# Layer norms of a transformer layer: VectorE reads the spread rows of 1/std and mean from PSUM

## The chip, the cores and the metric

The kernel runs on one core of one Trainium2 chip. The time is the device time of one execution in microseconds; less is better. The profile is one profiled execution on that core.

## The reference

One layer of a diffusion backbone on 1024 tokens of width 1024, all in fp32: modulation, two attention mixers (windowed and global) merged by gates, and a ConvFFN. Each of the two sublayers ends in a residual sum and a layer norm, which is the part that the change touches:

```
def _layer_norm(x, g, b):
    mu = mean(x, axis=-1)
    var = mean(square(x - mu), axis=-1)
    return (x - mu) * rsqrt(var + LN_EPS) * g + b

x = _layer_norm(DEEPNORM_ALPHA * x + gate1 * y, ln1_g, ln1_b)     # y: attention mixers
h = x * (1 + scale2) + shift2
u = conv1d(h @ w_up) + conv_b                                     # width 3, per channel
y = (silu(u_gate) * u_val) @ w_down
x = _layer_norm(DEEPNORM_ALPHA * x + gate2 * y, ln2_g, ln2_b)
```

## The kernel before

Activations lie transposed: features on the 128 partitions (8 tiles f = 0..7), tokens along the free dimension. A matrix product in fp32 is three matmuls on a high and a low fp32r part (`mm3`, L88 to L90); `split` makes the parts, the high one by a cast (L80) and the low one by a subtraction (L85).

A layer norm has to reduce over partitions. For a slice s of tokens, `ln_steps` (L1013) returns a list of steps. `stats`: matmuls of the running sums zs and zq against a column of ones give token sums (tile st), from which VectorE, with one power on GpSimd, makes rs = 1/std and mr = mean x rs per token. `diags`: VectorE multiplies the identity by rs and by mr (tiles dgr, dgm). `cast`: a matmul of ones against these spreads each row over all 128 partitions in PSUM (tiles bcr and bcm, or both halves of one tile bc where the slice has 256 tokens), and ScalarE copies each into SBUF (rb and mb, L1045). `apply(f)`, eight times: VectorE multiplies the tile z (zz in the second norm) by rb (L1050), VectorE or GpSimd subtracts mb (L1052), and `emit` does the rest. The argument pm says who subtracts: GpSimd where (f + 1) is a multiple of pm.

The first norm has three slices, LN1_S: tokens 0 to 511, 512 to 767, 768 to 1023, with pm = 2 throughout and the order f = 0, 4, 1, 5, 2, 6, 3, 7. It runs beside the matmuls of the attention's output projection (y_pair, tile y; its eviction is L1060) and of the first up-projection tiles (tile u). `emit1` stores a residual zo to the DRAM tensor zd (by ScalarE, or by GpSimd at L1094 for odd f), writes the high part B (L1068), and the low part by a subtraction on VectorE or GpSimd (L1074). Then `build` makes sums of tiles (t, T13, T24), on the same engines, for the following fast products.

The second norm has the slices LN2_S, of the same sizes. The first two use `ln_steps`, with pm from LN2_P; the third goes another way (token-major, tiles zt and stl) and is not touched. The first half, "b0", runs beside product 5 of the down-projection (tile p). `emit2` scales and shifts on ScalarE (tile of, L1407) and stores to the output (L1408). Then follow the products yl of the last quarter of the down-projection, one slice of 256 tokens after the other, each four feature tiles over 11 pairs of weights. Seven pairs are loaded early; the other four are cast by ScalarE (L80) and VectorE (L85) in a ring of four pairs of buffers that product 5 also uses. `accum` (L1414) evicts p and yl into zz on VectorE, and `sums` (L993, L994) updates zs and zq.

What sets the order: TensorE's instructions go in the order of the program (a manual schedule); the steps of a norm are put between matmuls by a clock of due times (`pend`, `tick`, LN1_F, LN1_D, LN2_D, LN2_E). On the other engines a planner orders the instructions by its own costs. Each engine then works its queue in order. [...]

Of the kernel before, what the change touches and what calls it, by code (L numbers as in the profile page):

```python
# [7 lines left out]
F32 = mybir.dt.float32  # L8
R32 = mybir.dt.float32r
AF = mybir.ActivationFunctionType  # L10
ALU = mybir.AluOpType
AX = mybir.AxisListType

P = 128
# [13 lines left out]
HALF = 512  # L28
# [26 lines left out]
PSU = 6, 7, 2, 3, 4, 5, 0, 1  # L55
PSO = 4, 5, 0, 1, 7, 6, 2, 3
UE = "vector", "vector", "vector", "vector", "vector", "gpsimd", "gpsimd"
LN2_P = 1, 2, 2
GAP = 1
LN1_S = slice(0, 512), slice(512, 768), slice(768, 1024)  # L60
VOFF = 0.0
# [6 lines left out]
def layer_kernel(  # L68
# [6 lines left out]
    nc = tc.nc  # L75
# [55 lines left out]
    def ht(name, shape=(P, T), dt=F32):  # L131
        hslot[name] = pool, tag = hfree.pop(0)
        return pool.tile(list(shape), dt, tag=tag, name=name, bufs=1)
# [71 lines left out]
    def modulate(k):  # L205
        wm, x, wr = st1.pop(k)
        w = wsplit(wr, f"qb{k}")
        for j in (0, 1):
            col = j * 8 + k
            mod(wm[j], sc, bmc[:, col:col + 1], modc[:, col:col + 1])  # L210
        hh = hTp.tile([P, T], R32, tag="hT", name=f"hh{k}", bufs=16)
        hl = hTp.tile([P, T], R32, tag="hT", name=f"hl{k}", bufs=16)
        a, b = modc[:, k:k + 1], modc[:, 8 + k:9 + k]
        for s in [slice(0, HALF), slice(HALF, T)] if k == 0 else [slice(0, T)]:
            nc.scalar.activation(hh[:, s], x[:, s], AF.Identity, bias=a, scale=b)
            nc.scalar.activation(x[:, s], x[:, s], AF.Identity, bias=a, scale=b)
            nc.vector.tensor_tensor(out=hl[:, s], in0=x[:, s], in1=hh[:, s].bitcast(F32), op=ALU.subtract)
        hT.append((hh, hl))
        return w
# [7 lines left out]
    w = modulate(0)  # L227
    for k in range(KT):
# [8 lines left out]
        w = wn  # L237
# [461 lines left out]
    for n, (gi, k) in enumerate(order):  # L699
# [9 lines left out]
        nm, src, tiles = groups[gi]  # L709
# [3 lines left out]
        w, c = ready.pop((gi, k))  # L713
        for t in tiles:
            if t < NT:
                s = slice(t * P, (t + 1) * P)
                a = hT[k][0][:, s], hT[k][1][:, s]
            else:
                s = slice((t - NT) * P, (t - NT + 1) * P)
                a = c[0][:, s], c[1][:, s]  # L720
# [161 lines left out]
    def big(name):  # L882
        return ps3.tile([P, T], F32, tag="big", name=name, bufs=3)

    def sml(name, w=512):
        return ps3.tile([P, w], F32, tag="sml", name=name, bufs=2)
# [28 lines left out]
    def zv(f, s):  # L915
        hf = s.start // HALF
        return zt_[f % 4, hf][:, f // 4, s.start - hf * HALF:s.stop - hf * HALF]
# [24 lines left out]
    for f in range(2, KT):  # L942
        bT[1, f] = ht(f"bT1_{f}")
        nc.sync.dma_start(bT[1, f], sgd[KT + f])
        w = wb[f // 2]
        ps = big(f"b1_{f}")
        for j in range(4):
            k = (f % 2) * 4 + j
            for hf in (0, 1):
                a = O[1, hf, 0, j // 2][:, j % 2], O[1, hf, 1, j // 2][:, j % 2]  # L950
# [9 lines left out]
    post = tc.alloc_tile_pool(name="post", bufs=1, side="left", reuse_waits="tile")  # L960
# [8 lines left out]
    def tiny(name):  # L969
        return post.tile([P, 8], F32, tag="tiny", name=name, bufs=6)  # L970

    def diag(cols, n, nm):
        dg = tm(f"dg{nm}", w=HALF).rearrange("p (a b) -> p a b", b=P)
        nc.vector.tensor_tensor(out=dg[:, 0:n], in0=ident.unsqueeze(1).to_broadcast([P, n, P]),
                                in1=cols.unsqueeze(2).to_broadcast([P, n, P]), op=ALU.mult)
        return dg[:, 0:n].rearrange("p a b -> p (a b)")
# [3 lines left out]
    def ln_flush():  # L980
        while sqs:
            sqs.pop(0)()
# [30 lines left out]
    def ln_steps(zs, zq, s, nm, emit, first, gap, gap1, gap2, each, pm=2, order=range(KT)):  # L1013
        w = s.stop - s.start
        n = w // P
        bcs = []
        sv = []

        def stats():
            ln_flush()  # L1020
            sv.extend(tiny(f"{a}{nm}") for a in ("mv", "m2", "rs", "mr"))
            mv, m2, rs, mr = sv
            st = sml(f"st{nm}")
            for t in range(n):
                ts = slice(s.start + t * P, s.start + (t + 1) * P)
                nc.tensor.matmul(st[:, t:t + 1], zs[:, ts], onec, start=True, stop=True)
                nc.tensor.matmul(st[:, n + t:n + t + 1], zq[:, ts], onec, start=True, stop=True)
            nc.vector.tensor_scalar(out=mv[:, 0:2 * n], in0=st[:, 0:2 * n], scalar1=1.0 / D, scalar2=None,
                                    op0=ALU.mult)
            nc.vector.tensor_tensor(out=m2[:, 0:n], in0=mv[:, 0:n], in1=mv[:, 0:n], op=ALU.mult)  # L1030
            nc.vector.scalar_tensor_tensor(out=rs[:, 0:n], in0=mv[:, n:2 * n], scalar=LN_EPS, in1=m2[:, 0:n],
                                           op0=ALU.add, op1=ALU.subtract)
            nc.gpsimd.tensor_tensor(out=rs[:, 0:n], in0=rs[:, 0:n], in1=mhalf[:, 0:n], op=ALU.pow)
            nc.vector.tensor_tensor(out=mr[:, 0:n], in0=mv[:, 0:n], in1=rs[:, 0:n], op=ALU.mult)

        def diags():
            bcs.extend(diag(c[:, 0:n], n, f"{a}{nm}") for a, c in zip("rm", sv[2:]))

        def cast():
            both = sml(f"bc{nm}") if 2 * w <= HALF else None  # L1040
            for i, a in enumerate("rm"):
                ps = sml(f"bc{a}{nm}")[:, 0:w] if both is None else both[:, i * w:(i + 1) * w]
                nc.tensor.matmul(ps, onesf, bcs[i], start=True, stop=True)
                o = post.tile([P, HALF], F32, tag="mrs", name=f"{a}b{nm}", bufs=2)[:, 0:w]
                nc.scalar.copy(o, ps)  # L1045
                bcs[i] = o

        def apply(f):
            zf = zv(f, s)
            nc.vector.tensor_tensor(out=zf, in0=zf, in1=bcs[0], op=ALU.mult)  # L1050
            e = nc.vector if (f + 1) % pm else nc.gpsimd
            e.tensor_tensor(out=zf, in0=zf, in1=bcs[1], op=ALU.subtract)  # L1052
            emit(f, s)

        return [(first, stats), (gap, diags), (gap1, cast)] + [(gap2 if n == 0 else each, lambda f=f: apply(f))
                                                for n, f in enumerate(order)]

# [421 lines left out]
    for p in (1, 6, 2, 7, 4, 5):  # L1479
# [35 lines left out]
        if p == 4:  # L1515
            after.append(lambda: pend.extend(ln_steps(zs2, zq2, h0, "b0", emit2, *LN2_D, LN2_P[0])))
    yb, ab = sides[nside[0] % 2], sides[nside[0] % 2 ^ 1]
# [10 lines left out]
    w = s.stop - s.start  # L1528
    nt = w // P

    def pst(n, name):
        return ps4.tile([P, HALF], F32, tag=f"r{n}", name=name)
# [50 lines left out]
    zt[0] = [pst(n, f"zt0_{n}") for n in yb[0:2]]  # L1583
    pend += ln_steps(zs2, zq2, r, "b1", emit2, *LN2_E, LN2_P[1])
    r = LN2_S[2]
    for f, done_ in enumerate(((4, 5), (6, 7, 0), (1,), (2, 3))):
        o = pst(yb[2 + f % 2], f"yl{f}_{r.start}")[:, 0:w]
# [15 lines left out]
    for t, a in OTO:  # L1603
        o = ot[t, a] = ht(f"ot{t}_{a}", (P, HALF))
        nc.vector.scalar_tensor_tensor(out=o, in0=lnr[0][:, a], scalar=mv[:, t:t + 1], in1=zt[a][t], op0=ALU.mult,
                                       op1=ALU.add)
    for t, a in OTO:
        o = ot[t, a]
# [125 lines left out]
```

## Time and profile before

| | |
|---|---|
| median of 3 runs | 1618.45 us (1617.10 to 1619.27) |
| profiled execution, first to last instruction | 1618.4 us; no other time of it is recorded, and this stands level with the median |
| TensorE busy | 1545.6 us, 95% |
| VectorE busy | 1199.0 us, 74% |
| ScalarE busy | 816.8 us, 50% |
| GpSimd busy | 746.4 us, 46% |
| granted TensorE clock, mean | 0.987 |

In the profile PE is TensorE (PEld its weight loads), DVE is VectorE, ACT is ScalarE, POOL is GpSimd and SP is SyncE, which issues most DMAs. "out<-in" are the program's names without numbers, and L1050 is line 1050 of the kernel. A row of a timeline has the start in us, the duration, engine, line, operation, operands and, in brackets, the idle time before it and what ended it. A row of a group has busy us and mean ns of one, then the idle time before. Matmuls are pipelined: a matmul's duration is longer than the distance to the next one's start.

### The profile page before, as it was taken

The page shows a single profiled execution, that of the slowest core. Times are in us where ns is not written, and L with a number is a line of the kernel's source. Part 1 is how long each engine was busy: PE and PEld are TensorE (multiplying, and loading weights), DVE is VectorE, ACT ScalarE, POOL GpSimd, SP SyncE. Part 2 cuts the span into 40 slices and gives each one's busy share as a digit, 9 for nine tenths or more (in the row PEclk, how much of TensorE's full clock was granted, in tenths as well). Part 3 has the DMA queues.
Part 4 walks back from the last instruction along what each step waited for, and adds up shares of the span by engine and source line. Part 5 has one row for each costly group of instructions (what it writes and reads, how often), then busy time and mean ns, then how long its engine had stood idle before and what let it go on. Part 6 is the DMA issues. An engine that isn't in the chain of part 4 may idle for free.

```text
span 1618.4 us, 22204 instructions
## 1 busy us (share of the span) xinstructions
PE 1545.6 (95%) x7748; PEld 1283.5 (79%) x7748; DVE 1199.0 (74%) x1764; ACT 816.8 (50%) x1455; POOL 746.4 (46%) x731
## 2 busy tenths in 40 slices
PE   6999999999999999999999988999999999999987
PEld 5878788888877887777788876888888888888877
DVE  7797646538887777888765786588888788658883
ACT  5422122458887667788332563444444444436542
POOL 0583302526666556555333444566667764111131
PEclk9999999999999999999999999999999999999997
DMA  9695662322246655520540313123334447996711
GB/s 377 218 322 179 212 203 85 124 72 60 63 132 146 148 126 129 119 63 19 196 169 18 109 46 116 66 105 104 117 105 118 115 119 202 342 268 228 230 64 53
DMA packets 112369, 230.00 MB, mean 142 GB/s; under 512 B 12961, under 2 KB 27809, under 8 KB 112161
## 3 DMA queue, kind: packets, MB, share of 16 engines
q1 hardware_dynamic: 96816, 198.93, 36.6%
q0 software_dynamic: 10400, 20.19, 8.1%
q10 hardware_dynamic: 5040, 9.46, 1.6%
q8 instruction: 61, 1.00, 0.2%
q14 instruction: 52, 0.42, 0.1%
HBM read 177.35 MB, written 65.86 MB: 150 GB/s over the span
## 4 chain that ended last, share of the span: by engine, by line
PE 78%; DVE 9%; ACT 4%; issue 4%; POOL 3%; DMA 2%; SPq 0%; DVEq 0%; ACTq 0%; POOLq 0%
PE ptr L529 5%; PE p L88 4%; PE p L89 4%; PE p L90 3%; PE g L88 3%; PE g L89 3%; PE g L90 3%; PE b L90 3%; PE b L89 3%; PE b L88 3%; PE c L88 2%; PE c L89 2%; PE c L90 2%; PE d L89 2%; PE d L90 2%
## 5 line engine op out<-in xcount | busy, mean ns | idle before, releaser
L539 DVE TENSOR_TENSOR ptl<-ptr,pth 128x512 fp32r<-128x512 f32 x188 | 124.8, 685 | 27.9 <-ACT pth L538 25.2
L529 PE MATMUL ptr<-ident,p 128*128 128x128 f32 x816 | 126.5, 278 | 10.1 <-DVE ptl L539 7.7
L538 ACT CAST pth<-ptr 128x512 fp32r<-128x512 f32 x188 | 106.5, 588 | 56.4 <-PE ptr L529 32.6
L85 DVE TENSOR_TENSOR ld<-rd,hd 128x1024 fp32r<-128x1024 f32 x77 | 94.2, 1241 | 51.1 <-ACT hd L80 49.0
L424 ACT ACTIVATE p<-p,nm 128x1024 f32<-128x1024 f32 (+2 forms) x128 | 125.4, 982 | 10.9 <-DVE p L457 10.1
L529 PEld LDWEIGHTS ptr<-ident,p 128*128 128x128 f32 x816 | 93.7, 140 | 40.1 <-DVE ptl L539 13.4
L80 ACT CAST hd<-rd 128x1024 fp32r<-128x1024 f32 x77 | 79.3, 1051 | 81.7 <-PE p L90 51.1
L550 PE MATMUL av<-pth,VT 128*128 128x512 f32 x236 | 104.6, 443 | 1.0 <-ACT avs L556 0.5
L88 PE MATMUL p<-hd 128*128 128x512 f32 x264 | 103.2, 391 | 0.0
L90 PE MATMUL p<-hd,ld 128*128 128x512 f32 x264 | 102.7, 389 | 0.0
L89 PE MATMUL p<-ld,hd 128*128 128x512 f32 x264 | 102.7, 389 | 0.0
L88 PE MATMUL g<-hh,whg 128*128 128x512 f32 x256 | 99.9, 390 | 0.0
L90 PE MATMUL g<-hh,wlg 128*128 128x512 f32 x256 | 99.8, 390 | 0.0
L551 PE MATMUL av<-ptl,VT 128*128 128x512 f32 x236 | 97.7, 414 | 2.0 <-POOL ptl L85 1.9
L89 PE MATMUL g<-hl,whg 128*128 128x512 f32 x256 | 99.6, 389 | 0.0
L85 POOL TENSOR_TENSOR wlg<-wg,whg 128x512 fp32r<-128x512 f32 x32 | 45.1, 1415 | 109.9 <-ACT whg L80 109.9
L457 DVE TENSOR_SCALAR_CACHE_REDUCE p<-s,cvt,nmc 128x1024 f32<-128x1024 f32 x64 | 84.4, 1339 | 12.4 <-PE s L413 12.0
L412 PE MATMUL s<-KL,q 128*128 128x512 f32 (+2 forms) x192 | 76.1, 396 | 2.9 <-ACT p_x L424 2.0
L186 DVE CUSTOM_DVE_ANT_0 wml<-wml,sc,bmc 128x1024 f32<-128x1024 f32 x32 | 45.0, 1418 | 39.7 <-DMA wml<-in_wmodT_dram 38.2
L82 POOL TENSOR_SCALAR pth<-prw 128x512 fp32r<-128x512 f32 x48 | 31.1, 647 | 88.3 <-ACT prw L535 62.7
L413 PE MATMUL s<-KL,q 128*128 128x512 f32 (+2 forms) x192 | 71.7, 373 | 0.0
L80 ACT CAST wA<-ru 128x512 fp32r<-128x512 f32 x57 | 35.5, 623 | 71.5 <-PE d L90 34.1
(420 smaller groups left out, 5022.9 us busy)
## 6 DMA issues: line engine op xcount, KB each, us to landing
wml<-in_wmodT_dram SPq DMA_DIRECT2D x48, 512.0 KB
ru<-in_w_up_dram SPq DMA_DIRECT2D x38, 512.0 KB
rd<-td SPq DMA_DIRECT2D x55, 256.0 KB
rd<-sd SPq DMA_DIRECT2D x44, 256.0 KB
rd<-in_w_dn_dram SPq DMA_DIRECT2D x33, 256.0 KB
wm<-in_wmodT_dram SPq DMA_DIRECT2D x16, 512.0 KB
wg<-in_w_g_dram SPq DMA_DIRECT2D x32, 256.0 KB
sgd<-sg ACTq DMA_DIRECT2D x32, 256.0 KB
```

The costliest lines, as they stand in the source:

```text
L80: nc.scalar.copy(hi, src)
L85: lo_eng.tensor_tensor(out=lo, in0=src, in1=hi.bitcast(F32), op=ALU.subtract)
L88: nc.tensor.matmul(ps, a[0], b[0], start=start, stop=False, skip_group_check=resumed)
L89: nc.tensor.matmul(ps, a[0], b[1], start=False, stop=False, skip_group_check=resumed)
L90: nc.tensor.matmul(ps, a[1], b[0], start=False, stop=stop, skip_group_check=resumed)
L424: nc.scalar.activation(p, s, AF.Exp, bias=nm[:, h:h + 1], scale=scale, accum_out=sm[:, h:h + 1])
L457: nc.vector.tensor_scalar(out=p, in0=o, scalar1=self.qscale(nqs)[:, hs] if self.br else -1.0, scalar2=self.other[:, hs], op0=ALU.mult, op1 ...
L529: nc.tensor.transpose(tr[:, h * P:(h + 1) * P], self.pslice(h, n), ident)
L538: nc.scalar.copy(hi, tr)
L539: nc.vector.tensor_tensor(out=lo, in0=tr, in1=hi.bitcast(F32), op=ALU.subtract)
L550: nc.tensor.matmul(self.av, v, hi, start=first, stop=False)
L551: nc.tensor.matmul(self.av, v, lo, start=False, stop=self.left == 0)
```

## The change

ScalarE no longer copies the spread row of 1/std: VectorE multiplies by it straight from PSUM. The spread mean row is still copied to SBUF, after both matmuls, since GpSimd subtracts from there; VectorE's own subtractions read it from PSUM. In the second norm's first half pm goes from 1 to 2: the four even tiles are subtracted on VectorE and the four odd ones on GpSimd, where all eight were on GpSimd. The tag "mrs" in SBUF, with two buffers, now takes one tile per norm slice instead of two.

```
-LN2_P = 1, 2, 2
+LN2_P = 2, 2, 2
...
             for i, a in enumerate("rm"):
                 ps = sml(f"bc{a}{nm}")[:, 0:w] if both is None else both[:, i * w:(i + 1) * w]
                 nc.tensor.matmul(ps, onesf, bcs[i], start=True, stop=True)
-                o = post.tile([P, HALF], F32, tag="mrs", name=f"{a}b{nm}", bufs=2)[:, 0:w]
-                nc.scalar.copy(o, ps)
-                bcs[i] = o
+                bcs[i] = ps
+            mean = post.tile([P, HALF], F32, tag="mrs", name=f"mb{nm}", bufs=2)[:, 0:w]
+            nc.scalar.copy(mean, bcs[1])
+            bcs.append(mean)

         def apply(f):
             zf = zv(f, s)
             nc.vector.tensor_tensor(out=zf, in0=zf, in1=bcs[0], op=ALU.mult)
-            e = nc.vector if (f + 1) % pm else nc.gpsimd
-            e.tensor_tensor(out=zf, in0=zf, in1=bcs[1], op=ALU.subtract)
+            if (f + 1) % pm:
+                nc.vector.tensor_tensor(out=zf, in0=zf, in1=bcs[1], op=ALU.subtract)
+            else:
+                nc.gpsimd.tensor_tensor(out=zf, in0=zf, in1=bcs[2], op=ALU.subtract)
             emit(f, s)
```

## The prediction

> **What bounds the kernel now.** I read the chain that ended last first, then the list of who waited for whom on TensorE, then the timelines around the two layer norms.
>
> ```profile
> span 1618.4 us, 22204 instructions
> ...
> PE 78%; DVE 9%; ACT 4%; issue 4%; POOL 3%; DMA 2%; SPq 0%; DVEq 0%; ACTq 0%; POOLq 0%
> ```
>
> TensorE carries 78% of the chain, so outside TensorE's idle gaps a faster VectorE or GpSimd is worth nothing. The gaps that touch the norms are these, in the columns total us, times, longest:
>
> ```profile
> PE yl L88 <- DVE zz L1414: 4.5, 1, 4.5
> PE u L88 <- DVE c L1233: 3.0, 1, 3.0
> PE sta L1026 <- DVE zs L993: 2.8, 1, 2.8
> PE u L89 <- DVE B L1074: 1.4, 1, 1.4
> PE u L89 <- POOL B L1074: 1.3, 1, 1.3
> PE bca L1043 <- ACT rba L1045: 1.3, 2, 0.8
> PE bcb L1043 <- ACT rbb L1045: 0.5, 1, 0.5
> ```
>
> The sum is 14.8 us, 0.9% of the span: this is nearly all the change can win directly. The largest lies behind the second norm's first half. Its timeline (start, duration, engine; "x8" is eight in a row):
>
> ```profile
> 1545.29 11.50 DVE L1050 TENSOR_TENSOR zz<-zz,rbb 128x512 f32<-128x512 f32 x8 [0.53 <-ACT rbb L1045]
> 1546.19 13.00 POOL L1052 TENSOR_TENSOR zz<-zz,mbb 128x512 f32<-128x512 f32 x8 [7.69 <-ACT mbb L1045]
> 1545.53 0.59 ACT L1045 COPY mbb<-bcmb 128x512 f32<-128x512 f32 x1 [0.27 <-PE bcmb L1043]
> 1559.23 0.82 ACT L1407 ACTIVATE of<-zz,ln2c 128x512 f32<-128x512 f32 x1 [0.44 <-POOL zz L1052]
> 1559.95 3.88 ACT L80 CAST hd<-rd 128x1024 fp32r<-128x1024 f32 x4
> 1561.01 4.63 DVE L85 TENSOR_TENSOR ld<-rd,hd 128x1024 fp32r<-128x1024 f32 x4 [2.32 <-ACT hd L80]
> 1574.91 0.48 DVE L1414 SCALAR_TENSOR_TENSOR zz<-yl,nmod,zz 128x256 f32<-128x256 f32 x1
> 1554.90 0.28 PE L88 MATMUL yl<-hd 128*128 128x256 f32 x1
> 1570.61 0.28 PE L90 MATMUL yl<-hd,ld 128*128 128x256 f32 x1
> 1575.44 0.58 PE L88 MATMUL yl<-hd 128*128 128x256 f32 x1 [4.55 <-DVE zz L1414]
> 1580.72 0.35 PE L88 MATMUL yl<-hd 128*128 128x256 f32 x1
> ```
>
> All eight subtractions run on GpSimd, back to back, 13.00/8 = 1.63 us each. ScalarE writes each feature tile out behind its subtraction, so the eighth output leaves at 1559.23, and only then do the four casts of the last weights start, in order behind it. VectorE, idle for 2.32 us, gets its first low part at 1561.01 and works off its backlog until it evicts the third accumulator at 1574.91. TensorE needs that bank and stands still from 1570.9 to 1575.44. GpSimd's subtractions thus set a gap 12 us later.
>
> The gap has a tail, seen in the granted clock (after the busy times: PEclk, DMA share, GB/s):
>
> ```profile
> 1574.00:1581.00 7.00, 5.56 (x26) 5.56 (x27) 3.36 (x9) 1.25 (x3) 0.00 (x0) 0.51 0.00 0
> 1585.00:1591.00 6.00, 6.00 (x30) 6.00 (x30) 0.06 (x1) 0.00 (x0) 0.00 (x0) 0.50 0.01 3
> ```
>
> After the gap TensorE gets half its clock: 25 matmuls take 1580.72 - 1575.44 = 5.28 us, where the same shape starts every 0.12 us before the gap (1554.90 to 1570.61 in 131 steps). That is 5.28 - 25 x 0.12 = 2.3 us more. The second slow stretch stands behind small statistics matmuls, not behind this gap, and I leave it as it is.
>
> **Why the operations are slow.** A multiply of the second norm takes 11.50/8 = 1.44 us. The nearest row of a VectorE subtraction that reads one input from PSUM, with GpSimd busy beside it, is the softmax stage's (min/median/max ns, then three in a row, then GpSimd's neighbour with its mean):
>
> ```profile
> L539 DVE TENSOR_TENSOR ptl<-ptr,pth x188: 652/686/695, 353.1 to 773.0; 128x512 fp32r<-128x512 f32 x188
> 400.08 1.88 DVE L539 TENSOR_TENSOR ptl<-ptr,pth 128x512 fp32r<-128x512 f32 x3
> L85 POOL TENSOR_TENSOR ptl<-prw,pth 128x512 fp32r<-128x512 f32 x48 | 63.4, 1320 | 2.6
> L1052 DVE TENSOR_TENSOR z<-z,mba 128x512 f32<-128x512 f32 x4 | 2.6, 683 | 0.0
> ```
>
> Not one of 188 is stretched (maximum 695 ns) and three take 1.88 us, so 0.60 us each in a row. The norm's multiply and GpSimd's subtraction both read two SBUF tensors, and both are stretched (1.44 against 0.69, 1.63 against 1.32): they hold each other up. With the row in PSUM, VectorE keeps one SBUF input.
>
> [...]
>
> **The change part by part.**
>
> *Second norm, first half* (rows above). Work added to VectorE: four subtractions. Twelve operations at 0.60, plus about 0.1 for the last to finish, are 7.3 us against 11.50. The first multiply no longer waits for ScalarE's copy: it can start at 1544.8 instead of 1545.29. VectorE is through at about 1552.3 (allowing 0.2 for the mean's matmul). GpSimd keeps four subtractions, one per 3 x 0.60 = 1.8 us, more than its 1.32, so it follows: the last ends at 1553.6. ScalarE's last output then ends at 1554.5 instead of 1560.0. The casts move 5.5 us earlier; the fourth needs the pair that TensorE frees at 1554.9 with the last matmul of product 5, which is in time. VectorE's backlog moves with them: the eviction of the third accumulator from 1574.91 to about 1569.5, before TensorE wants the bank at 1570.9. What is late next: that accumulator itself, whose matmuls end near 1569.4, so a gap of at most some tenths. Gain: 4.55, of which I keep 4.1, and the 2.3 of slow clock. Ends: nothing, and 6.9. I take 6.4, since the margin of 1.4 us covers an error of a quarter in the 5.5.
>
> *The cast, 256 wide* (first norm's parts 2 and 3, second norm's part 2):
>
> ```profile
> 923.00 0.70 PE L1043 MATMUL bca<-dgma,onesf 128*128 128x256 f32 x2 [0.82 <-ACT rba L1045]
> 938.50 0.70 PE L1043 MATMUL bca<-dgma,onesf 128*128 128x256 f32 x2 [0.46 <-ACT rba L1045]
> 1597.44 0.70 PE L1043 MATMUL bcb<-dgmb,onesf 128*128 128x256 f32 x2 [0.46 <-ACT rbb L1045]
> L1045 ACT COPY mba<-bca x2: 373/373/373, 923.7 to 939.2; 128x256 f32<-128x256 f32 x2
> ```
>
> Both rows lie in one bank, and TensorE's second matmul waits for the copy of the first. Without that copy these waits go: 0.82 + 0.46 on the path; the middle 0.46 falls into the later waits for VectorE (1.3, 1.4 and 3.0 us) and counts nothing. In exchange the first multiply may have to stand behind the mean's copy, if two engines may not read one bank together: 0.373 us, not on TensorE's path except in part 3. Gain 1.3, between 0.8 and 1.8.
>
> *First norm, first half.* GpSimd is continuously busy here and stretched (means, and min/median/max):
>
> ```profile
> L1074 POOL TENSOR_TENSOR B<-z,B 128x512 fp32r<-128x512 f32 x4 | 6.5, 1632 | 2.1 <-ACT z L1068 2.1
> L1052 POOL TENSOR_TENSOR z<-z,mba 128x512 f32<-128x512 f32 x4 | 6.4, 1588 | 0.7 <-DVE z L1050 0.7
> L1094 POOL TENSOR_SCALAR zo<-z,lnx x4: 770/1711/2234, 885.8 to 899.3; 128x512 f32<-128x512 f32 x4
> 899.52 0.82 ACT L1071 ACTIVATE zo<-z,lnx 128x512 f32<-128x512 f32 x1 [3.17 <-DMA zd<-zo]
> 900.89 0.69 DVE L994 TENSOR_TENSOR zq<-zq,sqa 128x512 f32<-128x512 f32 x1 [4.73 <-ACT sqa L992]
> 913.77 0.35 PE L1026 MATMUL sta<-onec,zs 128*128 128x1 f32 x2 [2.84 <-DVE zs L993]
> 914.00:919.00 5.00, 5.00 (x31) 5.00 (x31) 2.45 (x7) 1.04 (x1) 0.70 (x1) 0.66 0.02 6
> ```
>
> GpSimd's late zo is stored, ScalarE waits 3.17 us for that store to free the buffer, VectorE waits 4.73 us behind ScalarE, and runs from 900.89 without a pause to TensorE's 2.84 us wait. GpSimd's stretch is 4 x (1632 - 1320) + 4 x (1588 - 1320) + 4 x (1711 - 770) = 6.1 us. About half of VectorE's two-SBUF-input work there is the norm's own twelve operations, which leave; so some 3.0 us go, and the 2.84 with them if nothing else holds ScalarE. Ends 0 and 2.84 + 1.7 (the last row: 0.66 of the clock over 5 us behind the gap, 0.34 x 5); I take the middle of the wait, 1.4, because its chain passes four engines and a store.
>
> *First norm, last part.* VectorE's 938:945 rows:
>
> ```profile
> L1050 DVE TENSOR_TENSOR z<-z,rba 128x256 f32<-128x256 f32 x8 | 3.5, 484 | 2.9 <-ACT rba L1045 2.9
> L1052 DVE TENSOR_TENSOR z<-z,mba 128x256 f32<-128x256 f32 x4 | 2.6, 691 | 0.1
> ```
>
> At the unstretched 411 ns (the smallest of this shape) the twelve lose 8 x 73 + 4 x 280 = 1.7 us, less 0.37 if they wait for the mean's copy: 1.3 off the waits of 1.3, 1.4 and 3.0 that VectorE's stream sets. Ends 0 and 1.7. I take 1.4.
>
> *Banks.* PSUM rows now stay occupied until the last VectorE read. In the second norm they sit in two of the banks that the yl accumulators take: the second accumulator opens 21 matmuls after 1554.90, at 1557.4, and VectorE is through at 1552.3. Cost nothing; the cover is 5 us.
>
> Sum: -6.4 - 1.3 - 1.4 - 1.4 = -10.5 us. The span of 1618.4 stands level with the runs' median 1618.45, so the forecast is 1608.0 us.
>
> **The rivals.**
>
> *Only the second norm gains* (store and ScalarE's order keep the first norm's waits): -6.4, and 0.5 for its own cast wait, give 1611.5. For it: that wait is a store's. Against: the store is late because GpSimd is.
>
> *Hidden: the gap is refilled.* VectorE's order is chosen anew and the casts or evictions land where they were; only the first cast wait of 0.8 stays won: 1617.6. For it: the accumulator's own end leaves 1.4 us of margin. Against: 5.5 us are to be lost first.
>
> *Slower: the stretch stays.* If PSUM inputs did not free GpSimd, VectorE would do twelve at 1.44 = 17.3 us and end at 1562.1. The bank of the multiplier row, wanted at 1557.4, would hold TensorE for 4.7 us; VectorE's backlog ends 1.1 us later than now, and a second slow-clock stretch costs 2.3: 1618.4 + 1.1 + 2.3 = 1621.8. It decides once VectorE's last read comes after 1557.4. Against: L539's maximum of 695.
>
> [...]
>
> **How the numbers follow.** Forecast 0.58, only the second norm 0.22, hidden 0.13, slower 0.07. Within 0.2% (3.2 us) counts as no change, about what three runs that spread over 2 us can tell. Faster: 0.58 + 0.22 = 0.80; same 0.13; slower 0.07. The low end is every upper end, -6.9 - 1.8 - 4.5 - 1.7 = -14.9: 1603.5. The high end takes in the hidden case: 1617.6.
>
> **What would show it.** Multiplies at 0.69 us or less beside GpSimd; GpSimd's four at 1.3; the first of the four casts near 1554.5; no wait of yl for zz, clock 1.0 up to 1581; no wait of bca or bcb for ScalarE; sta's wait below 1.5. I am wrong if multiplies stay above 1 us, or if yl waits at its start for a bank.

## The result, and the profile after

| | before | after |
|---|---|---|
| median of the runs, beside each other | 1618.86 us (1614.97 to 1623.17, 6 runs) | 1602.42 us (1598.28 to 1604.46, 6 runs) |
| ratio after / before | | 0.9894, 95% interval 0.9877 to 0.9911 |
| profiled execution: time, span | 1618.4 us span | 1604.40 us, span 1602.6 us |

The change makes the kernel 1.1% faster. I forecast 1608.0 us and a low end of 1603.5: the direction was right, the gain of 16.4 us was larger than my largest. In every run on record the span is 1.7 to 2.3 us shorter than the time, so the profiled execution of before, with its span of 1618.4 us, took some 1620 us and does not stand level with the median; the two spans differ by 15.8 us.

First the chain that ended last, then TensorE's waits for other engines around the norms (total us, times, longest), both of the kernel after:

```profile
span 1602.6 us, 22190 instructions
...
PE 79%; DVE 8%; DMA 4%; ACT 4%; issue 3%; POOL 2%; SPq 0%; DVEq 0%; ACTq 0%; POOLq 0%
```

```profile
PE b L88 <- ACT T24h L1115: 6.5, 1, 6.5
PE u L89 <- DVE B L1077: 2.9, 1, 2.9
...
PE sta L1027 <- DVE zq L994: 0.2, 1, 0.2
```

The waits for zz (4.5), zs (2.8), c (3.0) and the casts (1.3 and 0.5) are gone; the two waits for B (1.4 and 1.3) have become one of 2.9. The wait for T24h was there before.

The second norm's first half, in the timeline of after (start, duration, engine, line, and the idle time before):

```profile
1536.78 1.88 DVE L1051 TENSOR_TENSOR zz<-zz,bcrb 128x512 f32<-128x512 f32 x3
1538.30 1.30 POOL L1055 TENSOR_TENSOR zz<-zz,mbb 128x512 f32<-128x512 f32 x1 [7.69 <-ACT mbb L1046]
1540.35 1.04 ACT L80 CAST hd<-rd 128x1024 fp32r<-128x1024 f32 x1
1543.36 0.68 DVE L1053 TENSOR_TENSOR zz<-zz,bcmb 128x512 f32<-128x512 f32 x1
1543.42 1.03 ACT L80 CAST hd<-rd 128x1024 fp32r<-128x1024 f32 x1
1543.52 1.30 POOL L1055 TENSOR_TENSOR zz<-zz,mbb 128x512 f32<-128x512 f32 x1 [0.37 <-DVE zz L1051]
1547.19 1.98 ACT L80 CAST hd<-rd 128x1024 fp32r<-128x1024 f32 x2
1548.26 2.36 DVE L85 TENSOR_TENSOR ld<-rd,hd 128x1024 fp32r<-128x1024 f32 x2 [0.57 <-ACT hd L80]
1558.72 0.48 DVE L1417 SCALAR_TENSOR_TENSOR zz<-yl,nmod,zz 128x256 f32<-128x256 f32 x1 [1.28 <-PE yl L90]
1561.60 0.48 DVE L1417 SCALAR_TENSOR_TENSOR zz<-yl,nmod,zz 128x256 f32<-128x256 f32 x1
1566.80 0.28 PE L1026 MATMUL stb<-onec,zs 128*128 128x1 f32 x2
```

Three multiplies in a row take 1.88 us beside a GpSimd that takes 1.30 us per subtraction: neither holds the other up. VectorE's twelve operations run from 1536.78 to 1544.04, the 7.3 us of the forecast. The eviction of the third accumulator lies 14.6 us behind the first yl (1547.00); before, it lay 20.0 us behind it (1574.91 - 1554.90). The order of ScalarE's queue is new as well: two of the four casts that stood behind the eighth output now stand between the outputs (1540.35 and 1543.42), and two behind it (1547.19). VectorE then has time to spare, for it waits 1.28 us for the first accumulator (1558.72). No run tells what the new order of the casts is worth beside the earlier outputs.

The first norm's first half, as groups with busy us, mean ns and idle time: first the rows of before that the prediction does not show, then after.

```profile
L1050 DVE TENSOR_TENSOR z<-z,rba 128x512 f32<-128x512 f32 x8 | 9.4, 1200 | 3.2 <-ACT rba L1045 3.2
...
L1094 POOL TENSOR_SCALAR zo<-z,lnx 128x512 f32<-128x512 f32 x4 | 6.4, 1606 | 0.2
...
L1071 ACT ACTIVATE zo<-z,lnx 128x512 f32<-128x512 f32 x4 | 3.2, 812 | 5.1 <-DMA zd<-zo 4.0 <-DVE z L1052 1.1
```

```profile
L1055 POOL TENSOR_TENSOR z<-z,mba 128x512 f32<-128x512 f32 x4 | 5.9, 1482 | 7.1 <-DVE z L1051 7.1
L1051 DVE TENSOR_TENSOR z<-z,bcra 128x512 f32<-128x512 f32 x8 | 5.2, 678 | 2.6 <-PE bcra L1043 2.6
...
L1097 POOL TENSOR_SCALAR zo<-z,lnx 128x512 f32<-128x512 f32 x4 | 3.5, 877 | 0.2
L1074 ACT ACTIVATE zo<-z,lnx 128x512 f32<-128x512 f32 x4 | 3.2, 805 | 1.8 <-DMA zd<-zo 1.8
...
L994 DVE TENSOR_TENSOR zq<-zq,sqa 128x512 f32<-128x512 f32 x3 | 2.2, 727 | 3.4 <-ACT sqa L992 3.4
```

VectorE's multiplies fall from 1200 to 678 ns, GpSimd's zo from 1606 to 877, ScalarE's wait for the store from 4.0 to 1.8 us in all.

Stage by stage the two profiles compare as follows. The marks are starts of TensorE's instructions. "Lost" is TensorE's busy time times (1 - granted clock), summed over windows of 1 us: the time that the slow clock took.

| stage | before, us (lost) | after, us (lost) | difference |
|---|---|---|---|
| start to first spread (bcra) | 876.3 (0.0) | 878.3 (3.4) | +2.0 |
| first to second spread | 45.3 (1.7) | 40.7 (0.0) | -4.6 |
| second to third spread | 15.9 (0.0) | 14.8 (0.0) | -1.1 |
| third spread to last u | 61.9 (3.1) | 57.7 (3.0) | -4.2 |
| last u to first yl | 555.5 | 555.5 | 0.0 |
| first yl to last spread (bcb) | 41.5 (6.1) | 34.3 (3.4) | -7.2 |
| last spread to last yl | 9.4 (0.0) | 8.6 (0.0) | -0.8 |
| last yl to end | 12.7 | 12.7 | 0.0 |

Ahead of the first spread nothing was changed; after lost 3.4 us to the slow clock there, before nothing.

### The profile page after: what moved, and what is told of

It is laid out like the page before. It is cut to its first block, busy times and chain, and to the rows that moved or that the text cites. A ratio compares the mean times of both kernels' runs of the same rounds, so it can differ in the third digit from the quotient of the medians.

```text
span 1602.6 us, 22190 instructions
## 1 busy us (share of the span) xinstructions
PE 1541.2 (96%) x7748; PEld 1281.7 (80%) x7748; DVE 1183.1 (74%) x1768; ACT 813.5 (51%) x1450; POOL 730.6 (46%) x727
## 4 chain that ended last, share of the span: by engine, by line
PE 79%; DVE 8%; DMA 4%; ACT 4%; issue 3%; POOL 2%; SPq 0%; DVEq 0%; ACTq 0%; POOLq 0%
PE ptr L529 5%; PE p L89 4%; PE p L90 4%; PE p L88 4%; PE b L90 3%; PE b L89 3%; PE b L88 3%; PE g L88 2%; PE g L89 2%; PE c L88 2%; PE c L90 2%; PE s L412 2%; PE c L89 2%; PE g L90 2%; PE av L550 2%
## 5 line engine op out<-in xcount | busy, mean ns | idle before, releaser
L457 DVE TENSOR_SCALAR_CACHE_REDUCE p<-s,cvt,nmc 128x1024 f32<-128x1024 f32 x64 | 84.4, 1339 | 12.3 <-PE s L413 11.8
L82 POOL TENSOR_SCALAR pth<-prw 128x512 fp32r<-128x512 f32 x48 | 31.0, 646 | 87.6 <-ACT prw L535 61.9
L80 ACT CAST wS<-s 128x512 fp32r<-128x512 f32 x76 | 45.8, 621 | 48.6 <-POOL s L1077 44.4
```

What stands on the lines that cost most here:

```text
L80: nc.scalar.copy(hi, src)
```

## The experiments

Times are ratios to runs of the kernel before on the same chip, turned into us at 1618.45. "Spread to spread" and the other stages are those of the table.

**e1: the first norm's first slice alone reads PSUM; e2: its other two slices alone.**

```
# e1 (e2: nm in ("a1", "a2")); elsewhere both rows are copied as before;
# apply is that of the changed kernel
-                o = post.tile(...); nc.scalar.copy(o, ps); bcs[i] = o
+                if not (nm == "a0"):
+                    o = post.tile(...); nc.scalar.copy(o, ps)
+                    ps = o
+                bcs[i] = ps
+            if (nm == "a0"):
+                mean = post.tile(...); nc.scalar.copy(mean, bcs[1]); bcs.append(mean)
```

> Only the first norm's first slice (tokens 0 to 511) reads its rows from PSUM; everything else is as before. Theory A (each part of the gain is made where its rows are read): the first half's stretch goes and TensorE's wait for the running sum (2.8 us) with its slow clock, 4.7 us between the spread of the first slice and that of the second; the stretch from the third slice's spread to the last up-projection matmul stays at 61.5 us. Time about 4.7 us below before (1614). Rival B (what the last part gained was carried over: the engines come out of the first half further ahead): that stretch falls to 57 us here too, time about 9 us below before (1609.5). Rival C (the planner's new order made the gain, not the reads): the multiplies get short (0.6 us) but sta's wait stays above 2 us, time within 1.5 us of before.

> Only the first norm's second and third slices (256 tokens each) read their rows from PSUM. Theory A: sta's wait stays 2.8 us; the cast wait of 0.82 goes; from the third slice's spread to the last up-projection matmul 61.5 us become 57; time 5 to 6 us below before (1613). Rival B (carried over from the first half): the stretch stays near 60.5 us (only the second cast wait of 0.46 and a few tenths of VectorE's go), time 1 to 2 us below before.

e1: ratio 0.9964 (0.9952 to 0.9976), -5.8 us. e2: 0.9971 (0.9957 to 0.9986), -4.7 us. TensorE's waits in e1:

```profile
PE yl L88 <- DVE zz L1422: 4.6, 1, 4.6
PE u L88 <- DVE c L1241: 2.7, 1, 2.7
PE u L89 <- DVE B L1082: 1.4, 1, 1.4
```

and in e2:

```profile
PE u L89 <- DVE B L1082: 2.9, 1, 2.9
PE sta L1026 <- DVE zs L993: 2.9, 1, 2.9
...
PE u L88 <- DVE c L1241: 0.4, 1, 0.4
```

Theory A holds: each gain is made where its rows are read. e1 loses the wait for zs and keeps those of the last part; e2 the other way round, and its two waits for B have already become one of 2.9. Nothing is carried over: the stage from the third spread takes 60.4 us in e1 and 57.3 in e2. Rival C falls with the wait for zs; that the order of VectorE's queue changed too, and what part it had, is taken up below. The windows behind the running sum's matmuls (start and end, length, busy us of PE, PEld, DVE, ACT and POOL, then granted clock, DMA share, GB/s) show what the wait drags along, first e1, then e2:

```profile
912.00:917.00 5.00, 5.00 (x37) 4.70 (x37) 3.90 (x11) 2.11 (x2) 0.70 (x1) 1.00 0.09 11
```

```profile
919.00:924.00 5.00, 5.00 (x27) 4.71 (x27) 3.50 (x8) 1.06 (x1) 0.00 (x0) 0.74 0.31 106
```

Full clock without the wait, 0.74 with it.

**e3: PSUM reads everywhere, all eight subtractions of the second norm's first half on GpSimd; e4: the sharing alone.**

```
e3, against the changed kernel:    e4, against the kernel before:
-LN2_P = 2, 2, 2                   -LN2_P = 1, 2, 2
+LN2_P = 1, 2, 2                   +LN2_P = 2, 2, 2
```

> All reads from PSUM as in the changed kernel, but all eight subtractions of the second norm's first half on GpSimd as before. Theory (two SBUF inputs on VectorE hold GpSimd up): GpSimd's eight take 8 x 1.32 = 10.6 us in place of 13.0, so the casts of the last weights come 2.4 us earlier and TensorE's wait for the third accumulator falls from 4.5 to about 2.2 us; with the first norm's 10 us and the last cast's 0.5 the time is about 13 us below before (1605.5). Rival (in the second norm only the sharing counts): that wait stays above 4 us, time about 10.5 us below before (1608).

> The sharing of the second norm's first half alone, all rows copied to SBUF as before. Theory (sharing without PSUM reads keeps the contention): VectorE's twelve operations stretch while GpSimd's four run: 6.5 us with 1.44 us each and the other seven or eight at 0.6, about 11 us in all, so it ends near 1556 and the casts come about 3 us earlier than before; the wait for the third accumulator falls from 4.5 to between 1 and 2 us, the slow clock behind it stays, time 3 to 4 us below before (1615). Rival (the sharing alone is the gain of the second norm): no wait for the third accumulator, clock full up to the end of that slice, time 7 us below before (1611.5).

e3: 0.9924 (0.9911 to 0.9936), -12.3 us. e4: 0.9974 (0.9962 to 0.9986), -4.2 us. The timeline of e3:

```profile
1537.90 4.87 DVE L1051 TENSOR_TENSOR zz<-zz,bcrb 128x512 f32<-128x512 f32 x8
1539.42 10.07 POOL L1055 TENSOR_TENSOR zz<-zz,mbb 128x512 f32<-128x512 f32 x8 [7.68 <-ACT mbb L1046]
```

and of e4:

```profile
1547.57 1.30 DVE L1050 TENSOR_TENSOR zz<-zz,rbb 128x512 f32<-128x512 f32 x2 [0.53 <-ACT rbb L1045]
1548.78 0.69 DVE L1052 TENSOR_TENSOR zz<-zz,mbb 128x512 f32<-128x512 f32 x1
1549.01 1.61 POOL L1052 TENSOR_TENSOR zz<-zz,mbb 128x512 f32<-128x512 f32 x1 [8.22 <-DVE zz L1050]
1549.38 2.39 DVE L1050 TENSOR_TENSOR zz<-zz,rbb 128x512 f32<-128x512 f32 x2
```

In e3 the eight subtractions take 10.07 us where they took 13.00, and the wait for the third accumulator falls from 4.5 to 1.6 us. In e4 each GpSimd subtraction (1.61 us) costs VectorE 1.1 us (two multiplies in 2.39 us, 1.30 where GpSimd is idle), and the wait falls to 1.3 us. So reads and sharing each take away about 3 us of the 4.5, and only both take it all. Both theories held, and the rivals are out by the waits (above 4 us in e3, none in e4); e3's wait fell further than the 2.2 I expected.

**e5: the second norm alone, reads and sharing.** The edit is that of e1 with the condition nm[0] == "b", and LN2_P = 2, 2, 2.

> Only the second norm reads from PSUM and shares its first half's subtractions; the first norm is as before. If the two norms add up: the whole change took 17.8 us (16.4 in the medians), the first norm's parts alone 5.8 and 4.7, so this should be 5.5 to 7 us below before (1612 to 1613.5). Theory for its size: the wait for the third accumulator (4.5 us) and the cast's wait (0.5) go, 5.0 us, and the slow clock behind that wait is no sure gain, since one slow stretch behind the small statistics matmuls stays. Rival (wait and slow clock go together, as the prediction had it): 7 us or more, and the stretch from the first yl matmul to the last slice's spread falls by 7 us against a kernel in which that wait of 4.5 us remains.

Ratio 0.9949 (0.9932 to 0.9966), -8.3 us (5.5 to 11.0). The window from the first yl to the last spread:

```profile
1553.00:1584.00 31.00, 31.00 (x266) 30.92 (x265) 17.75 (x38) 10.08 (x23) 1.11 (x2) 1.00 0.08 27
```

No wait and no slow clock at all in this execution: 31.3 us. It was not so in the two profiles of the changed kernel, which lost 3.4 and 1.7 us here (after, e12). By the time alone the theory (5.5 to 7) and the rival (7 or more) are not told apart. By the stage the rival came true in this execution: 31.3 us are 7.0 less than in e1 (38.3), where the wait remains, and 10.2 less than before.

**e6: rows in SBUF as before, but both matmuls first, then both copies.**

```
                 nc.tensor.matmul(ps, onesf, bcs[i], start=True, stop=True)
+                bcs[i] = ps
+            for i, a in enumerate("rm"):
                 o = post.tile(...)
-                nc.scalar.copy(o, ps)
+                nc.scalar.copy(o, bcs[i])
                 bcs[i] = o
```

> As before, but both matmuls of a spread first and then both copies into SBUF: only TensorE's waits for the first copy (0.82, 0.46 and 0.46 us) are taken away, nothing is read from PSUM by VectorE. Theory: the stretch from the second to the third slice's spread falls from 15.9 to 15.1 us, the last spread to the last yl from 9.4 to 8.9; the third wait is absorbed by VectorE's waits behind it; 1.3 us in all (1617.5). Rival (the cast wait is a larger part of the gain, since what follows it moves too): 2.5 us or more.

Ratio 0.9983 (0.9964 to 1.0002): -2.8 us, not told from 0 or from either expectation by the time. By the stages the cast's waits are worth more than I put them at: second to third spread 14.8 us instead of 15.9, last spread to last yl 8.6 instead of 9.4, as in the changed kernel, with nothing read from PSUM. And the planner ordered VectorE's queue in the last part anew, as in the changed kernel, which is worth another 1.8 us on the path (e8). By the stages the rival holds: 1.1, 0.8 and 1.8 are 3.7 us.

**e8: as before, with that order alone.**

```
+        ins = nc.vector.scalar_tensor_tensor(...)       # conv3, second operation
+        if not c00: c00.append(ins)
...
+            with tc.issue_after(c00[0].ins):            # build: s1 of k = 3, second sum of s2 of k = 2
                 sub(nc.vector, ...)
```

> As before, with all rows copied into SBUF, but VectorE's queue takes the order that the changed kernel has in the first norm's last part: two of the sums t (0.60 us each) stand behind the first convolution instead of ahead of it. Theory (of the 3.1 us by which that convolution ends earlier in the changed kernel, 1.2 are the order's and 1.9 the reads'): TensorE's wait for it falls from 3.0 to 1.8 us, time 1 us below before (1618). Rival 1 (the reads alone): it stays at 2.7 to 3.0. Rival 2 (the order alone): it falls below 0.5 us, time 3 us below before.

Ratio 0.9994 (0.9982 to 1.0007), -1.0 us, not told from 0. The wait for the convolution is 1.9 us, as the theory said; but it shrinks with slow clock ahead of it (1.6 us in e5, with the queue of before), so the end of the convolution decides. What sets this stage is the end of the first convolution's second operation (start plus 1.27), whose bank TensorE's next u needs (it waits 3.0 us for c in before). One row each of before, e8, e6 and after:

```profile
963.86 1.27 DVE L1233 SCALAR_TENSOR_TENSOR c<-u,cvt,c 128x1023 f32<-128x1023 f32 x1
```

```profile
966.52 1.28 DVE L1240 SCALAR_TENSOR_TENSOR c<-u,cvt,c 128x1023 f32<-128x1023 f32 x1
```

```profile
964.23 1.27 DVE L1235 SCALAR_TENSOR_TENSOR c<-u,cvt,c 128x1023 f32<-128x1023 f32 x1
```

```profile
935.21 0.42 DVE L1051 TENSOR_TENSOR z<-z,bca 128x256 f32<-128x256 f32 x1 [3.00 <-ACT mba L1046]
948.87 0.58 PE L89 MATMUL u<-B,hwu 128*128 128x256 f32 x1 [2.88 <-DVE B L1077]
957.05 1.27 DVE L1236 SCALAR_TENSOR_TENSOR c<-u,cvt,c 128x1023 f32<-128x1023 f32 x1
```

Counted from the third spread (937.45, 941.19, 939.61 and 933.74), the convolution ends after 27.7 us before, 26.6 in e8, 25.9 in e6 and 24.6 after. So 3.1 us were won. The order is worth 1.1 to 1.8 of them. The reads' part is what is left, 1.3 to 2.0: 1.3 is the difference between e6 and after, which have the same operations ahead of the convolution, though not in the same sequence. The prediction allowed 1.3 for the reads. Rival 1 and rival 2 are both out.

**e7: only the multiplies read PSUM; VectorE's subtractions read the mean's copy in SBUF.**

```
-                nc.vector.tensor_tensor(out=zf, in0=zf, in1=bcs[1], op=ALU.subtract)
+                nc.vector.tensor_tensor(out=zf, in0=zf, in1=bcs[2], op=ALU.subtract)
```

> The changed kernel, but VectorE's own subtractions read the mean from its copy in SBUF; only the multiplies read PSUM. Theory (each VectorE operation with two SBUF inputs that meets GpSimd costs both): the multiplies stay at 0.6 to 0.68 us, VectorE's subtractions that meet GpSimd take 1.2 to 1.45 us in place of 0.6, the second norm's twelve operations 8 to 9 us in place of 7.3; the time is 1 to 3 us above the changed kernel (1603.5 to 1605.5). Rival (the multiplies alone made the contention): same as the changed kernel within 1 us (1602.5).

Ratio 0.9914 (0.9893 to 0.9934). The timeline of the second norm's first half:

```profile
1539.99 1.88 DVE L1051 TENSOR_TENSOR zz<-zz,bcrb 128x512 f32<-128x512 f32 x3
1541.79 2.17 DVE L1053 TENSOR_TENSOR zz<-zz,mbb 128x512 f32<-128x512 f32 x2
1544.70 4.80 POOL L1055 TENSOR_TENSOR zz<-zz,mbb 128x512 f32<-128x512 f32 x3 [1.89 <-DVE zz L1051]
```

The operations do what the theory says: the multiplies stay at 0.6 us; of VectorE's four subtractions two, beside GpSimd's, take 1.56 and 0.87 us, and the other two 0.68; three of GpSimd's in a row need 1.6 us each; and the twelve end after 8.3 us instead of 7.3. The time does not decide: 1604.07 us lies in the theory's range, but the ratio of 0.9914 is level with the 0.9912 of the changed kernel in e12. TensorE's stages around them are the changed kernel's (first to second spread 40.7 us, first yl to last spread 31.3 with no slow clock), so no wait has come back. For the stretch the theory holds; that the path loses nothing by it is the rival's forecast, but not for the rival's reason.

**e9 to e12: tiles of their own, the convolution ahead, both, and the changed kernel again.** e9 takes `both` only for names that begin with "b"; e10 puts t13 of k = 2 and 3, t24 of k = 2, T24l of k = 0 and T13l of k = 1 behind the first convolution, by the edit of e8; e11 is both.

> The changed kernel, but the two spread rows of the first norm's 256-token slices lie in PSUM tiles of their own, so that the first multiply need not stand behind the mean's copy. Theory: VectorE's first multiply comes 1.0 us after the spread in place of 1.5, the first convolution 0.4 us earlier, the wait for it shorter by that; time 0 to 0.5 us below the changed kernel, which no timing can tell, so the rows decide. Rival: the planner orders the queue anew and loses it again.

> The changed kernel, but in the first norm's last part VectorE's queue has the first convolution ahead of the sums t of tiles 2 and 3 and of two low parts T. Theory (the end of this part is set by VectorE's stream up to that convolution, 24.6 us after the third spread, plus 32.6 us of matmuls): the convolution ends 3 to 4 us earlier, the wait for it (0 to 1.9 us by the clock) is gone, the stretch to the last u falls from 57.3 us (without slow clock) to 55.5; 1 to 2 us below the changed kernel. Rival: the sums that were put back are late for the products behind them and the wait for T24h (6.5 us) grows by as much.

> Both: rows in tiles of their own and the first convolution ahead. Theory: as with the order alone, and up to 0.4 us less; 1 to 2 us below the changed kernel (1600.5 to 1601.5). Rival: no better than the order alone, since the wait for the low part B (2.9 us), which stands ahead of the convolution, then sets the part.

> The changed kernel itself once more, beside the three kernels made from it. Theory for its clock: without TensorE's wait for the running sum there is no slow clock between the first and the second spread (0 us lost there, 1.7 us in before); without the wait for the third accumulator the slow clock in the yl stage costs 0 to 3.4 us, by chance; time 1600 to 1604.

Ratios, all beside the same runs of before: e12 0.9912 (0.9898 to 0.9926), e9 0.9908 (0.9895 to 0.9921), e10 0.9945 (0.9925 to 0.9966), e11 0.9938 (0.992 to 0.9956). In e9 VectorE starts 0.63 us after the third spread instead of 1.47:

```profile
937.91 1.08 DVE L1051 TENSOR_TENSOR z<-z,bcra 128x256 f32<-128x256 f32 x3 [2.62 <-PE bcra L1043]
```

and the stage takes 56.6 us against 57.3 in e12 (lost to the clock 1.6 and 1.4): 0.7 us less, which the time (1602.78 against 1603.02) cannot tell. e12 itself came as expected: no slow clock between the first and the second spread, 1.7 us of it in the yl stage, 1603.02 us. In e10 the wait for the convolution is gone; with 3.0 us lost to the slow clock the stage takes 57.8 us. e11's stage falls to 54.4 us, below what the theory had, but the rival named for e10 wins in both: the wait for T24h grows. In e11 the largest wait, and what the last of the casts waits for:

```profile
PE b L88 <- ACT T24h L1120: 14.7, 1, 14.7
```

```profile
1007.49 1.04 ACT L1120 CAST T24h<-t 128x1024 fp32r<-128x1024 f32 x1 [9.63 <-DMA td<-c]
```

It is 14.7 us in e10 too. In e11 2.9 us were won ahead of it and 8.1 lost here (14.7 against 6.6 in e12): no version beat the changed kernel measurably. An order that takes the convolution ahead without delaying that store was not tried.

## Why the prediction was right or wrong

The mechanism was right, and all rivals fell. Multiplies at 0.6 us, GpSimd at 1.3, no wait for zz, for the cast, or for zs: each sign came as listed, but for two. The clock was to be full up to 1581, and was not; and of the casts two came earlier than forecast, in a new order of ScalarE's queue. Nor does a price of the read from PSUM show: a 128x512 multiply takes 0.68 us from there (after), and 0.69 from SBUF while GpSimd stands still (before). What failed are sizes, the two largest in the first norm, and in both I held the order of VectorE's queue fixed.

*First norm, first half: forecast -1.4, measured -4.6.* This is the step that failed. I took half the wait of 2.84 because its chain passes four engines and a store, and counted the slow clock of 1.7 only in the end of the range. But the chain handed everything on. One row of before that the prediction does not show, then the chain after:

```profile
895.50 1.30 POOL L1094 TENSOR_SCALAR zo<-z,lnx 128x512 f32<-128x512 f32 x1
```

```profile
892.29 1.21 POOL L1097 TENSOR_SCALAR zo<-z,lnx 128x512 f32<-128x512 f32 x1
896.22 0.81 ACT L1074 ACTIVATE zo<-z,lnx 128x512 f32<-128x512 f32 x1 [1.80 <-DMA zd<-zo]
897.59 0.69 DVE L994 TENSOR_TENSOR zq<-zq,sqa 128x512 f32<-128x512 f32 x1 [2.28 <-ACT sqa L992]
```

Counted from the first spread (876.29 and 878.27), GpSimd's third zo ends at 20.5 us before and at 15.2 after, ScalarE's wait for a store ends at 23.2 and 18.0 (2.3 us after SyncE issued ScalarE's previous zo, right behind GpSimd's, in both), VectorE's wait for ScalarE at 24.6 and 19.3. That is 5.3 us at every link, more than the wait of 2.84, so there was nothing to halve. GpSimd's shorter work is 2.1 of the 5.3 (12.1 us after, 14.3 before, from its first subtraction to the end of that zo). The other 3.2 are order: VectorE's queue now has the third multiply ahead of VectorE's own first subtractions, so GpSimd's first subtraction starts 3.1 us behind the spread instead of 6.2. All eight profiles whose first slice reads PSUM have the new order, the other six the old one. No run has the reads with the old order here, so this split is read off two traces and not tested.

GpSimd's relief itself was sized about right: 4 x (1588 - 1482) + 4 x (1606 - 877) gives 3.3 us, nearly all of it in zo, and I said 3.0 (half of 6.1, a sum that mixes a median of 1711 with means). VectorE's multiplies got 8 x (1200 - 678) = 4.2 us shorter as well, which I left out; but VectorE still waits for ScalarE behind them (4.73 us before, 2.28 after), so ScalarE set its restart. And here the slow clock belongs to the wait: in the six profiles with it (before, e2, e4, e5, e6, e8) 1.7 us or more were lost in this stage, in the eight without it (after, e1, e3, e7, e9 to e12) nothing.

*First norm, last part: forecast -1.4, measured -3.1 for the path.* The reads were priced about right (1.3 forecast, 1.3 to 2.0 measured), and the 0.37 for the mean's copy was near: VectorE starts 1.47 us behind the third spread instead of 1.03. The rest is order: the planner put two sums behind the convolution, and I held its order fixed, except as a danger. This is the one term that came out well beyond the end of its range (1.7). The two profiles differ by 4.2 us here, since before holds 1.6 us of slow clock behind the wait for c as well, and after 0.5 of its own beyond the path of 24.6 + 32.7 us; e1, with the queue of before, took 60.4.

*The cast: forecast -1.3, measured -1.9* (1.1 and 0.8). The row of a wait counts idle time only; the distance between the two matmuls fell by 1.41 - 0.43 = 0.98 and 1.06 - 0.43 = 0.63.

*Second norm, first half: forecast -6.4, measured -7.2 in the two profiles.* The 4.5 are firm: clear of slow clock this stage takes 35.4 to 35.9 us in the five profiles with the wait (before, e1, e2, e6, e8) and 30.9 to 31.3 in the seven without (after, e5, e7, e9 to e12). The slow stretch at the end of the wait is firm too: 1.5 to 2.7 us were lost in it in each of those five (I had 2.3), and nothing there in the seven. What varies is the second slow stretch: 3.4 us lost in before and in after, 1.7 in e10 and e12, none in the other eight. In the changed kernel's own profile it came with no wait at all:

```profile
1569.40:1576.10 6.70, 6.70 (x33) 6.70 (x34) 0.59 (x2) 0.00 (x0) 0.00 (x0) 0.50 0.01 2
```

It stands behind the small statistics matmuls that start at 1566.80. That stretch I had seen and left as it is; the profile of before happened to hold both. In all, 1.5 to 6.1 us (mean 2.8) were lost in the five profiles with the wait and 0 to 3.4 (mean 1.0) in the seven without, so the slow clock is worth 1.8 us on average. That my 6.4 stands so near the 4.5 + 1.8 is in part luck, since it left the second stretch out.

With the measured sizes the sum is -4.6 - 1.9 - 3.1 - (4.5 + 1.8) = -15.9 us; the two measurements of the changed kernel gave -17.2 (0.9894) and -14.2 (0.9912), which is -15.7 on average. The low end of the range missed the median by 1.1 us: it was the sum of upper ends, and the upper end of the last part (1.7) held the reads without the order.

The contention itself shows in e3, e4 and before: a 128x512 multiply on VectorE with one SBUF input takes 0.61 us beside GpSimd's subtractions, and each of those 1.26 us (e3); with two SBUF inputs, a pair of multiplies takes 1.1 us more with one GpSimd subtraction beside it (e4). In before, the mean of 1.44 us mixes two multiplies of 0.69 us, which start before GpSimd does, and six of 1.78 us that start 1.70 us apart, near the sum of one multiply and one subtraction (0.61 and 1.26 us, 4.87/8 and 10.07/8 in e3). In e7 VectorE's two subtractions with two SBUF inputs that met GpSimd's took 1.56 and 0.87 us, the other two 0.68.

## What to carry to other kernels

Where VectorE and GpSimd work side by side and an operand of VectorE comes out of PSUM anyway, leave it there: the copy is saved, and neither engine stretched the other here (0.61 us a multiply and 1.26 us a subtraction in e3, 1.44 and 1.63 in before). When a stretch goes, follow the relief link by link along the chain that feeds the waiting engine (here GpSimd, a store, ScalarE, VectorE); where it exceeds the wait and no link has something else to wait for, expect the whole wait to go, and do not halve it for the length of the chain; here the slow clock behind it went too (1.7 us or more in each of the six profiles with the wait for zs, nothing in the eight without). Look at the stage's path (here a convolution queued behind sums) before pricing only the waits, for a planner may queue it anew, as it did here in three places; and moving work behind the path (e11) pays only until its own consumer waits.

## What was unexpected of the hardware

The slow clock comes in pieces. In the clock records of all fourteen traces every slow stretch lasts 3.41 us or a multiple of it (6.83 and 10.24 in before and after, 17.07 in e10 and e11), but for the one that runs to the end of each trace. One piece at half clock costs 1.7 us where TensorE is busy throughout (from 915.3 in before), and less where it also waits (1.4 us from 952.8 in before). The number of pieces changes from run to run in the same code (0 to 5.1 us were lost ahead of the first spread, where nothing was changed: 0.0 in before, 3.4 in after). Six runs of the kernel before differ by 8 us. At least one piece stood behind the wait of 2.8 us for zs, with its small matmuls, in each of six profiles; behind the wait of 2.9 us for B none stood in e3 (0.0 lost in that stage), and the waits of 1.3 and 1.6 us for zz (e4, e3) were followed by 8 us of full clock. What brings a piece stays open.
